# V's products taken from x * g, u written over it afterwards, and the first stage's rows, root, splits and bias sums placed anew

## The chip, the cores and the metric

The kernel runs on one core of a Trainium2 chip. The metric is the time that the device takes for one execution, in microseconds (us). Engines are named as the profile names them: PE is TensorE, PEld its weight loads, DVE VectorE, ACT ScalarE, POOL GpSimd, SP SyncE, which here only issues transfers (DMA).

## What is computed

One layer of a decoder block over 1024 tokens of width 1024. Only the start of it matters here: the normalised and modulated input `u`, its projections, and attention.

```python
def _modulate(x, g, shift, scale):
    return _rmsnorm(x, g) * (1 + scale[:, None, :]) + shift[:, None, :]
...
mod = c_act @ w_ada[l] + b_ada[l]
sh1, sc1, gt1, sh2, sc2, gt2 = jnp.split(mod, 6, axis=-1)
u = _modulate(h, g_mix[l], sh1, sc1)
...
proj = u @ w_in
q, k, v, us, g_att, g_ssm = jnp.split(proj, ...)
```

Three attention patterns with a softmax over the keys follow, an S5 branch, gates, an output projection, and a gated MLP. With r the inverse root mean square of a token and g = g_mix * (1 + scale), u = x * g * r + shift. So u @ W = r * ((x * g) @ W) + shift @ W: a product with x * g can be scaled by r per token afterwards, and the shift adds one row, the same for all tokens. The weights of a softmax sum to one, so such a row in V adds itself unchanged to the output of attention.

## The kernel before

Every float32 matrix product is done as three products of reduced-precision parts: high times high, high times low, low times high (`mm3`, L188 to L192). So each operand is split into a high part (ScalarE, a copy) and a low part (VectorE or POOL, a subtraction).

**First products.** `xT` is x with channels on partitions, in eight tiles of 128 channels (`xs[k]`). For each k, `xg[k]` is x * g in two parts. g needs the row products of the conditioning vector with `w_ada` (`row_dot`, L1502, one VectorE row per 128 outputs). The first products take 128 columns each of q, k and the two thirds of `us` (seven tiles in PSUM, `b0`: four columns groups, two halves of 512 tokens, less one) from `xg`, k by k, with the weights `w0` (L416 to L453).

**Root.** x by token (`xn`, eight blocks) is squared and summed on ScalarE (L356). `root` (L394) makes r from it; `spread_a` and `spread_b` (L406 to L414) spread r along the free axis with diagonal tiles and a product with -1 (L413), so `rr` holds -r (signs cancel in what follows).

**Shift row.** The eight `row_dot`s for the shift stand in the table `DOTS` among the first products; `shl` holds the shift in two parts, and 16 short products with `w0` (L494, L495) give shift @ W for q, k and us.

**u and V.** `u_half` makes u for one k and half: VectorE (L1480), ScalarE for the high part (L1481), VectorE for the low part (L1486). V's products follow, tokens as rows: for each half (`hf`) and each k, four tiles of 128 tokens, 12 products, 192 in all. In the first half u is made one k ahead; in the second half u's second half is made, and the q and k tiles are scaled, biased and split (`put_q`, `put_k`), and V's tiles of the first half are emptied (`put_v`: four ScalarE rows, L531, and four VectorE rows, L534, for each tile of 128 tokens). The four tiles of the second half follow, then the `us` tiles (`put_us`, L568).

**Attention** then runs with a fill of further projections from u; its first fill products take a PSUM bank that V's fifth tile must have left. Weights for these go through `Weights` (L70 to L140): one load buffer, a high part on ScalarE, and a low part on POOL (L121) for the first ones.

**Order.** The program is recorded by hand in the order of this code; each engine runs its rows strictly in that order and waits by semaphore. `b.unit(us)` moves a clock that lets spawned generators issue their next piece. SP's transfers are one queue in program order too.

Of the kernel before, what the change touches and what calls it, by code (L numbers as in the profile page):

```python
# [16 lines left out]
P = 128  # L17
# [35 lines left out]
DOTS = ((4, 5), (5, 1), (5, 4), (6, 0), (6, 2), (6, 4), (6, 6), (7, 1))  # L53
# [16 lines left out]
class Weights:  # L70
# [25 lines left out]
    def _split_to(self, n):  # L96
        b, nc = self.b, self.b.nc
        while self.ns < min(n, len(self.items)):
# [10 lines left out]
            lo = nc.vector if self.ns >= self.vec else nc.gpsimd  # L109
# [105 lines left out]
def body(tc, I, O, dbg=None):  # L215
    b = Builder(tc, I, O)
    nc = tc.nc
    with ExitStack() as ctx:
# [88 lines left out]
        def split_w(i):  # L307
            raw = raws.pop(i)
            w = b.whl.tile([P, 2, 1024], R32, name="whl", tag="whl") if i == 5 else b.A([P, 2, 1024], R32, "whA")
            nc.scalar.activation(w[:, 0], raw, AF.Copy)  # L310
            nc.vector.tensor_sub(w[:, 1], raw, w[:, 0].bitcast(F32))
            return w
# [27 lines left out]
        ssq = pg1.tile([P, 2, KT], F32, name="ssq")  # L340
# [7 lines left out]
        def load_xn(n):  # L348
            if n in (0, 2):
                page = b.A([P, 2, D], F32, "xn")  # L350
                xnp[n], xnp[n + 1] = page[:, 0], page[:, 1]
            nc.sync.dma_start(xnp[n % 4], I["xn"][n])

        def square(n):

            nc.scalar.activation(xnp[n % 4], xnp[n % 4], AF.Square, accum_out=ssq[:, 0, n:n + 1])  # L356
# [37 lines left out]
        def root(_):  # L394
# [6 lines left out]
            nc.vector.scalar_tensor_tensor(r, t, -1.5, r, op0=OP.add, op1=OP.mult)  # L401

# [12 lines left out]

        late = {}  # L416
        for fn, at in ((row_dot, DOTS), (root, ((7, 0),)), (spread_a, ((7, 2),))):
# [6 lines left out]
        for k in range(KT):  # L424
# [4 lines left out]
            if 3 <= k < 7:  # L429
                load_row(2 * k - 6)  # L430
                load_row(2 * k - 5)
            if 2 <= k < 6:
                for n in (2 * k - 4, 2 * k - 3):
                    if n > 3:
                        square(n - 4)
                    load_xn(n)
# [4 lines left out]
            elif k == 6:  # L441
                for n in range(4, KT):
                    square(n)
                load_w(4)
                load_w(5)
            o = (k % 2) * 512
            for n, ((t, hf), ps) in enumerate(b0.items()):
# [3 lines left out]
                b.mm3(ps, w[:, 0], w[:, 1], xg[k][:, 0, halves[hf]], xg[k][:, 1, halves[hf]], k == 0, k == KT - 1)  # L451
                b.unit(0.65)
            del xg[k]  # L453
        spread_b(0)
# [3 lines left out]
        u = []  # L458
        t0 = {}
        for e in range(2):  # L460
            page = b.A([P, 4, HF], F32, "t0")
            for j in range(4):
                t0[2 * e + j // 2, j % 2] = page[:, j]
        del page

        def scale_r(*ii):
            for i in ii:
                nc.vector.tensor_mul(t0[i], b0.pop(i), rr[:, halves[i[1]]])
# [9 lines left out]
        def u_half(k, hf, *between):  # L478
            u_a(k, hf)
            scale_r(*between)  # L480
            u_b(k, hf)
# [1507 lines left out]
```

## Time and profile before

| | us |
|---|---|
| three timed runs | 1149.85, 1153.71, 1154.62 |
| their median | 1153.71 |
| profiled execution, whole | 1151.12 |
| its span in the profile | 1149.3 |
| TensorE busy | 1108.6 (96%) |
| VectorE busy | 866.3 (75%) |
| ScalarE busy | 583.2 (51%) |
| POOL busy | 149.6 (13%) |
| granted TensorE clock, mean | 0.99 |

A row of a timeline gives start, length, engine, line, operation, tiles written and read, and in brackets the idle time ahead of it with what ended it. Rows of one engine overlap a little: the next may start before the last has ended. "x4" are four rows in one. TensorE's busy time counts modelled ends of overlapping products, so that a share of 96% doesn't mean that it is never behind.

### The profile page before, as it was taken

How to read it: one execution, taken by the hardware profiler on the slowest of the kernel's cores; microseconds unless marked ns; L12 is line 12 of the kernel's file. 1: busy time of each engine (PE TensorE's matmuls, PEld its weight loads, DVE VectorE, ACT ScalarE, POOL GpSimd, SP SyncE). 2: the span in 40 equal slices, each digit the busy share in tenths (PEclk: the TensorE clock that was granted, in tenths of full speed). 3: DMA queues.
4: the chain of work that ended last, by engine and by line, in shares of the span. 5: the costliest groups of instructions: out<-in, count | busy, mean ns of one | idle time of the engine just before them, and what ended most of it. 6: DMA issues, size and time to landing. Idle time of an engine off the chain costs nothing.

```text
span 1149.3 us, 14742 instructions
## 1 busy us (share of the span) xinstructions
PE 1108.6 (96%) x5286; PEld 912.2 (79%) x5286; DVE 866.3 (75%) x1656; ACT 583.2 (51%) x1065; POOL 149.6 (13%) x171
## 2 busy tenths in 40 slices
PE   9799999999999999999799999999999999999995
PEld 8667888888878887878678887788888888887784
DVE  6678687876569597378686879888877677879876
ACT  3648777778832312243233665443444346636653
POOL 1001444445422222000000000000000000000003
PEclk9999999999999999999999999999999999999998
DMA  9811111111022122245484362245423327779433
GB/s 366 351 55 56 63 39 38 47 46 65 11 72 85 49 83 64 65 137 185 163 316 148 104 238 73 92 152 203 139 92 129 128 92 274 251 265 386 142 128 147
DMA packets 57337, 159.20 MB, mean 139 GB/s; under 512 B 7440, under 2 KB 13712, under 8 KB 55472
## 3 DMA queue, kind: packets, MB, share of 16 engines
q1 hardware_dynamic: 47520, 144.56, 35.2%
q10 hardware_dynamic: 9744, 13.70, 3.8%
q8 instruction: 41, 0.67, 0.2%
q14 instruction: 32, 0.26, 0.1%
HBM read 126.20 MB, written 31.46 MB: 137 GB/s over the span
## 4 chain that ended last, share of the span: by engine, by line
PE 62%; DVE 14%; DMA 8%; ACT 8%; issue 8%; POOL 1%; SPq 0%; POOLq 0%; ACTq 0%; DVEq 0%
PE ps_s L1333 10%; PE ps_mm L1333 9%; PE ps_mm L190 7%; PE ps_t L1333 7%; PE ps_mm L192 7%; PE ps_mm L191 7%; PE ps_s L192 2%; PE ps_s L190 2%; PE ps_s L191 2%; DMA xn<-in_xn 2%; PE ps_t L1641 2%; PE ps_s L1605 1%; PE ps_o L1658 1%; PE ps_s L1606 1%; DMA x<-in_xT 1%
## 5 line engine op out<-in xcount | busy, mean ns | idle before, releaser
L1333 PE MATMUL ps_s<-op,half 128*128 128x512 f32 x792 | 189.6, 390 | 4.0 <-ACT ps_s L1347 2.9
L1333 PEld LDWEIGHTS ps_s<-op,half 128*128 128x128 f32 x792 | 148.3, 188 | 36.5 <-ACT ps_s L1347 3.9
L190 PE MATMUL ps_mm<-u,whl 128*128 128x512 f32 x360 | 144.9, 402 | 3.2 <-ACT sg L744 2.0
L192 PE MATMUL ps_mm<-u,whl 128*128 128x512 f32 x360 | 141.6, 393 | 0.0
L191 PE MATMUL ps_mm<-u,whl 128*128 128x512 f32 x360 | 141.1, 392 | 0.0
L1333 PE MATMUL ps_mm<-op,half 128*128 128x512 f32 x528 | 125.2, 389 | 0.0
L1333 PEld LDWEIGHTS ps_mm<-op,half 128*128 128x128 f32 x528 | 99.1, 188 | 20.6
L1333 PE MATMUL ps_t<-op,half 128*128 128x512 f32 x432 | 103.9, 389 | 0.7 <-ACT tp L1341 0.7
L1333 PEld LDWEIGHTS ps_t<-op,half 128*128 128x128 f32 x432 | 81.0, 188 | 17.9 <-ACT tp L1341 1.1
L121 POOL TENSOR_TENSOR whl<-wraw,whl 128x256 fp32r<-128x256 f32 (+2 forms) x52 | 62.1, 1196 | 208.1 <-ACT whl L118 208.1
L1447 POOL TENSOR_TENSOR hh<-hh,acc 128x512 f32<-128x512 f32 x3 | 4.3, 1454 | 650.9 <-ACT acc L1436 650.9
L190 PEld LDWEIGHTS ps_mm<-u,whl 128*128 128x128 f32 x360 | 68.2, 189 | 15.3 <-ACT sg L744 2.5
L192 PEld LDWEIGHTS ps_mm<-u,whl 128*128 128x128 f32 x360 | 67.9, 189 | 15.4 <-DVE whl L121 0.3
L191 PEld LDWEIGHTS ps_mm<-u,whl 128*128 128x128 f32 x360 | 68.3, 190 | 10.5
L1646 DVE TENSOR_TENSOR PT<-ps_t,PT 128x512 fp32r<-128x512 f32 (+1 forms) x80 | 50.6, 633 | 28.2 <-ACT PT L1644 27.7
L1139 DVE TENSOR_TENSOR half<-scr,half 128x512 fp32r<-128x512 f32 x80 | 54.5, 684 | 16.2 <-ACT half L1138 16.1
L118 ACT ACTIVATE whl<-wraw 128x256 fp32r<-128x256 f32 (+2 forms) x72 | 48.7, 676 | 28.3 <-PE ps_s L192 14.6
L1617 ACT ACTIVATE S<-S,mcol 128x128 f32<-128x128 f32 (+3 forms) x64 | 49.3, 771 | 14.5 <-DVE mcol L1615 12.9
L1621 POOL TENSOR_SCALAR S<-S,mcol 128x128 f32<-128x128 f32 (+3 forms) x64 | 48.7, 764 | 49.8 <-DVE mcol L1620 35.6
L1138 ACT ACTIVATE half<-scr 128x512 fp32r<-128x512 f32 x80 | 49.0, 625 | 8.7 <-DVE scr L1120 5.6
L1139 DVE TENSOR_TENSOR half<-wraw,half 128x512 fp32r<-128x512 f32 x66 | 45.0, 685 | 8.0 <-ACT half L1138 7.9
L1644 ACT ACTIVATE PT<-ps_t 128x512 fp32r<-128x512 f32 (+1 forms) x80 | 43.8, 551 | 10.5 <-PE ps_t L1641 9.4
(516 smaller groups left out, 2424.7 us busy)
## 6 DMA issues: line engine op xcount, KB each, us to landing
wraw<-in_wup SPq DMA_DIRECT2D x32, 512.0 KB, 3.6
fq<-f SPq DMA_DIRECT2D x16, 1024.0 KB, 5.3
ft<-fq SPq DMA_DIRECT2D x14, 1024.0 KB, 7.7
ada<-in_wada SPq DMA_DIRECT2D x24, 512.0 KB, 8.9
wraw<-in_wdn SPq DMA_DIRECT2D x20, 512.0 KB, 5.8
adaB<-in_wada ACTq DMA_DIRECT2D x16, 512.0 KB, 4.5
wraw<-in_wout SPq DMA_DIRECT2D x16, 512.0 KB, 3.7
hd<-h SPq DMA_DIRECT2D x12, 512.0 KB, 7.3
```

The lines of the kernel that those rows point to most:

```text
L118: nc.scalar.activation(w[:, 0, cs], raw[:, cs], AF.Copy)
L121: lo.tensor_sub(w[:, 1, cs], raw[:, cs], w[:, 0, cs].bitcast(F32))
L190: nc.tensor.matmul(ps, wh, xh, start=first, stop=False)
L191: nc.tensor.matmul(ps, wh, xl, start=False, stop=False)
L192: nc.tensor.matmul(ps, wl, xh, start=False, stop=last)
L1138: nc.scalar.activation(w[:, 0], src, AF.Copy)
L1139: lows.append(lambda: nc.vector.tensor_sub(w[:, 1], src, w[:, 0].bitcast(F32)))
L1333: mm = lambda wp, xp, i: nc.tensor.matmul(ps, w[:, wp, ws], xp[:, cs], start=first and k + i == 0, stop=k == KT // 2 - 1 and i == 2, skip_ ...
L1617: nc.scalar.activation(tl, tl, AF.Exp, bias=mc[:, 0:1], scale=-1.0, accum_out=mc[:, 2:3])
L1621: nc.gpsimd.tensor_scalar(tl, tl, mc[:, 3:4], 0.0, op0=OP.mult, op1=OP.add)
L1644: nc.scalar.activation(pt[:, 0, :w], tps[:, :w], AF.Copy)
L1646: 0, lambda: nc.vector.tensor_sub(pt[:, 1, :w], tps[:, :w], pt[:, 0, :w].bitcast(F32)))
```

## The change

1. V's products read `xg[k]` and not u. So they can start when the first products end. `put_v` scales each tile by r per token: ScalarE's copy takes `scale=ssq[:, 2, t]` (a column, r with the sign that it needs, one small row more in `root`), VectorE's subtraction becomes a `scalar_tensor_tensor` with the same column. The shift's part of V is a row of its own: `rows_of("v", wv)`, 16 more short products, transposed into the columns `vb`, added in attention where the two halves of an output are summed.
2. `u` is the same memory as `xg`. `gen_u`, spawned, writes each k and half after V's products have read it (`taken`).
3. The seven PSUM tiles of the first products are copied to SBUF by ScalarE as they end (`keep`), so that V's tiles get these banks; the scaling by r then works on the copies.
4. Loads: the blocks of x by token come without a wait for each other (four pages in place of two), ahead of the shift's rows. V's first weight is loaded and split among the first products. `DOTS` keeps four of the eight row dots; four move into V's first half, with the two spreads, the scaling, the shift and both `rows_of`.
5. The low parts of the first two weights for attention go to VectorE, not POOL. Of the `us` tiles, three are written among V's last emptyings, bias and layout in one row.

```diff
-DOTS = ((4, 5), (5, 1), (5, 4), (6, 0), (6, 2), (6, 4), (6, 6), (7, 1))
+DOTS = ((6, 1), (6, 4), (7, 2), (7, 4))
+U_PACE = 1.5
...
-            lo = nc.vector if self.ns >= self.vec else nc.gpsimd
+            lo = nc.vector if self.ns >= self.vec or self.ns < 2 else nc.gpsimd
...
+            nc.vector.tensor_scalar(ssq[:, 2], r, -1.0, None, op0=OP.mult)
...
+        def keep(i, ps):
+            if not t0_pages:
+                t0_pages.extend(b.A([P, 4, HF], F32, "t0") for _ in range(2))
+            t0[i] = t0_pages[i[0] // 2][:, 2 * (i[0] % 2) + i[1]]
+            nc.scalar.activation(t0[i], ps, AF.Copy)
...
-        for fn, at in ((row_dot, DOTS), (root, ((7, 0),)), (spread_a, ((7, 2),))):
+        for fn, at in ((row_dot, DOTS), (low4, ((7, 0),)), (root, ((7, 1),)), (spread_a, ((7, 5),)), (more_rows, ((6, 6),))):
...
+            for n in {2: (0, 1), 3: (2, 3), 4: (4, 5), 5: (6, 7)}.get(k, ()):
+                load_xn(n)
+            for n in {4: (0, 1), 5: (2, 3), 6: (4, 5)}.get(k, ()):
+                square(n)
+            if k == 5:
+                load_w(4)
+            for n in {5: (0, 1), 6: (2, 3)}.get(k, ()):
+                load_row(n)
...
+                if k == KT - 1:
+                    keep((t, hf), ps)
...
+        u = [xg[k] for k in range(KT)]
...
+        def gen_u():
+            last = None
+            for hf in range(2):
+                for k in range(KT):
+                    while (k, hf) not in taken:
+                        yield 0.6
+                    u_a(k, hf)
+                    if last:
+                        u_b(*last)
...
+                    last = k, hf
+                    yield U_PACE
...
+        def rows_of(n, ws, tag="o"):
+            ps = b.ps(tag)
+            for k in range(KT):
+                o = (k % 2) * 512
+                w = ws[k // 2][:, :, o:o + 512]
+                nc.tensor.matmul(ps[0:2], shl[:, k], w[:, 0], start=k == 0, stop=False)
+                nc.tensor.matmul(ps[0:1], shl[:, k, 0:1], w[:, 1], start=False, stop=k == KT - 1)
+                b.unit(0.43)
+            brow[n] = b.tp()
+            nc.scalar.activation(brow[n][0:2], ps[0:2], AF.Copy)
...
-                nc.scalar.activation(V[p][:, t, :, 0:HD], src[:, 2 * p:2 * p + 2], AF.Copy)
-            yield
+                nc.scalar.activation(V[p][:, t, :, 0:HD], src[:, 2 * p:2 * p + 2], AF.Copy, scale=ssq[:, 2, t:t + 1])
+            yield 1.4
...
-                nc.vector.tensor_sub(V[p][:, t, :, HD:P], src[:, 2 * p:2 * p + 2], V[p][:, t, :, 0:HD].bitcast(F32))
+                nc.vector.scalar_tensor_tensor(V[p][:, t, :, HD:P], src[:, 2 * p:2 * p + 2], ssq[:, 2, t:t + 1],
+                                               V[p][:, t, :, 0:HD].bitcast(F32), op0=OP.mult, op1=OP.subtract)
...
+                nc.scalar.activation(o, t0.pop((2 + m, hf)).rearrange("p (j t) -> p t j", t=T), AF.Identity,
+                                     bias=bias0[:, 2 + m:3 + m])
...
+                    if k == 1:
+                        load_w(7)
+                        spread_b(0)
+                        spread_a(1)
+                        row_dot(4)
+                        scale_r((1, 0))
+                        row_dot(5)
+                    if k == 2:
+                        spread_b(1)
+                        wv.append(split_w(6))
+                        row_dot(6)
+                        scale_r((2, 0))
+                        row_dot(7)
+                        shift()
+                        b.spawn(gen_u(), 0.5)
+                    if k == 3:
+                        scale_r((0, 0))
+                    if k == 4:
+                        rows_of("u", w0)
...
+                    if k == 6:
+                        scale_r((2, 1))
+                        rows_of("v", wv)
...
-                    if k + 1 < KT:
-                        u_b(k + 1, 1)
-                    next(put)
-                    if k + 2 < KT:
-                        u_a(k + 2, 1)
-                    list(put)
-                    xs[k] = None
-                    if k == 3:
-                        us0 = [(t - 2, hf, add_bias0(t, hf)) for t, hf in ((2, 0), (2, 1), (3, 0))]
+                    b.spawn(put)
+                    if k in (4, 5, 6):
+                        put_us(*((0, 0), (0, 1), (1, 0))[k - 4])
...
-            nc.vector.tensor_add(t[hp, 256:512], o[0:64, 0:256], t[0:64, 0:256])
+            nc.vector.scalar_tensor_tensor(t[hp, 256:512], o[0:64, 0:256], vb[0:64, 2 * p + h2:2 * p + h2 + 1], t[0:64, 0:256],
+                                           op0=OP.add, op1=OP.add)
```

Line numbers shift by the change: the spread's product is L413 before and L416 after, u's three rows are L1480, L1481, L1486 before and L1542, L1543, L1548 after, V's are L531 and L534 before and L567 and L570 after.

On TensorE, the end of the first products (the last tile, `ps_o`) and what follows it before (`tp,nones` is the spread, `shl` the shift, `ps_s` V's first tile):

```order
L190 MATMUL ps_o<-xg,whA 128x512
L191 MATMUL ps_o<-xg,whA 128x512
L192 MATMUL ps_o<-xg,whA 128x512
L413 MATMUL ps_o<-tp,nones 128x512
L494 MATMUL ps_o<-whl,shl 2x512
L495 MATMUL ps_o<-whl,shl 1x512
```

and with the change, from the same place on:

```order
L191 MATMUL ps_o<-xg,whA 128x512
L192 MATMUL ps_o<-xg,whA 128x512
L193 MATMUL ps_o<-xg,whA 128x512
L191 MATMUL ps_s<-whA,xg 128x512
L192 MATMUL ps_s<-whA,xg 128x512
L193 MATMUL ps_s<-whA,xg 128x512
```

V's products stand directly behind the first products now; the spread comes after V's first step of twelve, the shift's row after the fourth.

On VectorE, the emptying of V at the end of V's products before (`V<-` are V's rows, tiles 2 to 7 in banks t, mm and o; `u` and `x` rows make u; the last row is attention's first score):

```order
L534 TENSOR_TENSOR V<-ps_s,V 128x2x64 x4
L1486 SCALAR_TENSOR_TENSOR u<-x_103,mod,u 128x512
L534 TENSOR_TENSOR V<-ps_t,V 128x2x64 x8
L534 TENSOR_TENSOR V<-ps_mm,V 128x2x64 x8
L534 TENSOR_TENSOR V<-ps_o,V 128x2x64 x8
L1608 ISA S_939,mcol<-ps_s,near 128x128
```

and with the change (`xg` is u now, `whl<-wraw` a weight's low part for attention):

```order
L570 SCALAR_TENSOR_TENSOR V<-ps_t,ssq,V 128x2x64 x4
L122 TENSOR_TENSOR whl<-wraw,whl 128x1024
L1542 SCALAR_TENSOR_TENSOR x_102<-x_102,gs_115,rr 128x512
L1548 SCALAR_TENSOR_TENSOR xg<-xk,mod,xg 128x512
L570 SCALAR_TENSOR_TENSOR V<-ps_t,ssq,V 128x2x64 x4
L570 SCALAR_TENSOR_TENSOR V<-ps_mm,ssq,V 128x2x64 x8
L1542 SCALAR_TENSOR_TENSOR x_103<-x_103,gs_115,rr 128x512
L1548 SCALAR_TENSOR_TENSOR xg<-x_102,mod,xg 128x512
L1548 SCALAR_TENSOR_TENSOR xg<-x_103,mod,xg 128x512
L570 SCALAR_TENSOR_TENSOR V<-ps_o,ssq,V 128x2x64 x8
L1670 ISA S_970,mcol<-ps_s,near 128x128
```

A weight's split and the rows of u's last tiles now stand among V's last emptyings.

More of the change, by code (lines that the diff above doesn't have):

```diff
@@ L308, in split_w @@
             raw = raws.pop(i)
-            w = b.whl.tile([P, 2, 1024], R32, name="whl", tag="whl") if i == 5 else b.A([P, 2, 1024], R32, "whA")
+            w = b.whl.tile([P, 2, 1024], R32, name="whl", tag="whl") if i == 7 else b.A([P, 2, 1024], R32, "whA")
             nc.scalar.activation(w[:, 0], raw, AF.Copy)
@@ L441, in body @@
             elif k == 6:
-                for n in range(4, KT):
+                for n in (6, 7):
                     square(n)
-                load_w(4)
+                w4 = split_hi(4)
+                wv = [w4[0]]
                 load_w(5)
@@ L502, in body @@
[L502 to L513 removed]
+        taken = set()
@@ new lines, in gen_u @@
+        def gen_u():
[7 more added lines that the diff above has]
+                        u_b(*last)
+                    if last and last[1]:
+                        xs[last[0]] = None
+                    last = k, hf
+                    yield U_PACE
+            yield 0.7
+            u_b(*last)
+            xs[last[0]] = None
@@ new lines, in bias_cols @@
+        def bias_cols(n, width, out, tag="o"):
+            cps = b.ps(tag)
+            row = brow.pop(n)
+            for t in range(HF // width):
+                nc.tensor.transpose(cps[:width, 2 * t:2 * t + 2], row[0:2, t * width:(t + 1) * width], ident[0:2, 0:2])
+            bcp = b.tp()
+            m = 2 * HF // width
+            nc.scalar.activation(bcp[:width, :m], cps[:width, :m], AF.Copy)
+            yield 2.0
+            nc.vector.tensor_add(out[:width], bcp[:width, 0:m:2], bcp[:width, 1:m:2])
@@ L615, in body @@
                 vps += [b.ps(t) for t in ("mm", "mm", "o", "o")]
+        for t in (4, 5):
+            list(put_v(t))
+        b.drain()
+        for t in (6, 7):
+            list(put_v(t))
         p1.close()
@@ L625, in body @@
         W.prefetch(1)
-        for t in range(4, 8):
-            list(put_v(t))
-        for x in us0:
-            put_us(*x)
-        t0.clear()
-        del us0, x
+        assert not t0
         def U(k, hf):
@@ L693, in body @@
         W.slow = True
-        attention(b, V, QK, Oat, pS, near, far, ident, mcol, fill)
+        attention(b, V, QK, Oat, pS, near, far, ident, mcol, vb, fill)
         W.finish()
@@ L1570, in s5_coefficients, with attention @@
     v.tensor_scalar(AA[64:P, 1], AA[64:P, 1], -1.0, None, op0=OP.mult)
-def attention(b, V, QK, Oat, pS, near, far, ident, mcol, fill):
+def attention(b, V, QK, Oat, pS, near, far, ident, mcol, vb, fill):
     nc = b.nc
```

110 lines of the change are left out of this document (44 added, 66 removed).

## The prediction

> **What bounds the kernel now.** I read the busy time by stage first, with stages cut where TensorE's work changes.
>
> ```profile
> core 0: us, PE busy (x) PEld busy (x) DVE busy (x) ACT busy (x) POOL busy (x), PEclk, DMA share, GB/s
> 49.20:61.67 12.47, 6.66 (x20) 2.06 (x19) 6.52 (x14) 6.94 (x14) 0.00 (x0) 0.73 0.39 148
> 61.67:109.20 47.53, 46.09 (x199) 36.23 (x197) 39.28 (x68) 30.52 (x64) 3.71 (x2) 1.00 0.11 38
> 109.20:332.00 222.80, 218.46 (x1281) 186.16 (x1280) 153.82 (x464) 167.50 (x367) 99.14 (x132) 1.00 0.15 50
> ```
>
> The third row is attention: TensorE is busy for 98% of it, so a shift of its start reaches the end of the kernel nearly whole. Nothing behind it is changed in order. The second row is V's products. The first row is the gap between the first products and V's, which the change goes for. The timeline of TensorE gives its length, the waits what ends it:
>
> ```profile
> 48.98 0.39 PE L192 MATMUL ps_o<-xg,whA 128*128 128x512 f32 x1
> 54.48 2.08 PE L413 MATMUL ps_o<-tp,nones 128*128 128x512 f32 x2 [5.12 <-ACT tp L408]
> 61.67 0.40 PE L190 MATMUL ps_s<-whA,u 128*128 128x512 f32 x1
> 61.90 0.39 PE L191 MATMUL ps_s<-whA,u 128*128 128x512 f32 x1
> ...
> 65.96 1.02 PE L413 MATMUL ps_o<-tp,nones 128*128 128x512 f32 x2
> ...
> 110.34 0.47 PE L190 MATMUL ps_mm<-u,whl 128*128 128x512 f32 x1 [1.14 <-DVE V L534]
> ```
>
> A product starts 0.228 us after the one before it (61.67, 61.90). First products end at 48.98 + 0.23 = 49.2, V's start at 61.67: **12.5 us** apart, filled by the wait for the root, its spread over the partitions (L413) and 16 short products for the bias row (L494, L495). At 110.34 TensorE restarts for attention, held 1.14 us by VectorE's emptying of V's bank. **110.34 is the time to beat.**
>
> **The change on TensorE.** V's products now read x * g, which lies there, so they start at 49.2. They are 2 x 8 steps of 12: 192 x 0.2275 = 43.7. The two spreads move inside: 0.9 each (two passes; the row at 65.96 ran undisturbed). The bias row's 16 products stay and 16 more come for V's own shift row: 32 x 0.23 = 7.4. Small transposes: about 0.6. With no wait TensorE ends V at 49.2 + 43.7 + 1.8 + 7.4 + 0.6 = 102.7 and restarts, after the 1.2 that emptying the last bank cost before, at 103.9. That is **6.4 us earlier than 110.34**, the most the change can give. The extra row eats 3.7 of the gap.
>
> **Inputs.** SP's order is equal up to the last x, and then the eight blocks of x by token come before the rows for the shift.
>
> ```profile
> 25.53 1.56 SPq L297 DMA_DIRECT2D ada<-in_wada  x2
> 32.99 1.57 SPq L352 DMA_DIRECT2D xn<-in_xn  x2
> 39.12 1.57 SPq L352 DMA_DIRECT2D xn<-in_xn  x2
> 48.57 1.06 ACT L356 ACTIVATE xn<-xn 128x1024 f32<-128x1024 f32 x1 [3.23 <-DMA xn<-in_xn]
> 50.82 1.28 ACT L397 ACT_TABLE_LOAD   x1
> 50.99 1.23 DVE L1502 CUSTOM_DVE_ANT_0 ada<-ada,cpage 128x1024 f32<-128x1024 f32 x1 [3.01 <-DMA ada<-in_wada]
> 58.17 1.23 DVE L311 TENSOR_TENSOR whA<-wvx,whA 128x1024 fp32r<-128x1024 f32 x1 [3.36 <-ACT whA L310]
> ```
>
> Blocks of 512 KB go out every 1.24 us (six from 25.53 to 32.99) and land 9.5 us later (39.12 to 48.57). The six blocks of x by token that remain take the places from 25.53 on, so the last goes out at 31.7 and lands near 41.2; before, it landed near 49.7. The squares end near 44. The first V weight lands next (42.5), and VectorE has split it by 47.8; the table load and root sit between the seven bank copies that ScalarE now makes. None of this holds TensorE at 49.2. The next limit is VectorE: between 48.5 and the shift it has six row dots and two splits, with two root copies and the second spread of ScalarE in between. Laid end to end (a dot 1.2 and a split 1.14, as rows overlap the next by 0.08; two scalings 0.62; the shift's three small rows 0.6; waits for ScalarE's splits 3.2) the shift is ready at **63.1**. TensorE reaches the shift row at 49.2 + 4 x 2.73 + 1.8 = 62.0, so it waits **1.1**. If the last of these loads take the full 9.5 us after issue, 0.6 more. V's first half, with all that lies in it, then ends at 82.0, the second at 103.8 on TensorE.
>
> **The change on VectorE and ScalarE.** This decides. u is now made behind V's products, 16 tiles of 128x512, each a VectorE row, a ScalarE row and a VectorE row; before, it was made ahead of them. I count with these rows of VectorE's timeline (start, length):
>
> ```profile
> 59.31 0.75 DVE L1480 SCALAR_TENSOR_TENSOR xk<-xk,gs,rr 128x512 f32<-128x512 f32 x1
> 59.98 0.68 DVE L468 TENSOR_TENSOR t<-ps_s,rr 128x512 f32<-128x512 f32 x1
> 80.49 0.75 DVE L1480 SCALAR_TENSOR_TENSOR x<-x,gs,rr 128x512 f32<-128x512 f32 x1
> 82.69 0.75 DVE L1480 SCALAR_TENSOR_TENSOR xk<-xk,gs,rr 128x512 f32<-128x512 f32 x1
> 87.89 0.68 DVE L546 SCALAR_TENSOR_TENSOR QS<-t,QS 64x512 fp32r<-64x512 f32 x1
> 94.93 0.42 DVE L561 CAST KH<-KH 64x512 fp32r<-64x512 f32 x1
> 109.32 1.66 DVE L534 TENSOR_TENSOR V<-ps_mm,V 128x128 fp32r<-128x128 f32 x8
> ```
>
> and these of ScalarE's, then two groups by line and form (busy time, mean ns of one) and POOL's split:
>
> ```profile
> 53.15 1.28 ACT L408 ACTIVATE tp<-ident,ssq 128x128 f32<-128x128 f32 x4 [0.49 <-DVE ssq L401]
> 56.60 0.60 ACT L414 ACTIVATE rr<-ps_o 128x512 f32<-128x512 f32 x1 [2.17 <-PE ps_o L413]
> 88.37 0.73 ACT L1481 ACTIVATE u<-xk,mod 128x512 fp32r<-128x512 f32 x1
> 89.00 0.71 ACT L519 ACTIVATE t<-t,bias 128x512 f32<-128x512 f32 x1
> 89.74 0.63 ACT L543 ACTIVATE QS<-t 64x512 fp32r<-64x512 f32 x1
> 99.74 1.05 ACT L118 ACTIVATE whl<-wraw 128x1024 fp32r<-128x1024 f32 x1
> 100.69 0.75 ACT L531 ACTIVATE V<-ps_s 128x128 fp32r<-128x128 f32 x4
> 110.88 2.51 ACT L568 ACTIVATE usr<-t 128x512 f32<-128x512 f32 x2
> L408 ACT ACTIVATE tp<-ident,ssq 128x128 f32<-128x128 f32 x8 | 2.5, 389 | 0.5 <-DVE ssq L401 0.5
> L531 ACT ACTIVATE V<-ps_s 128x128 fp32r<-128x128 f32 x8 | 1.5, 283 | 0.0
> 100.87 2.41 POOL L121 TENSOR_TENSOR whl<-wraw,whl 128x1024 fp32r<-128x1024 f32 x1 [95.71 <-ACT whl L118]
> ```
>
> In the second half ScalarE first waits for the last tile of the first half to be read (82.0), with the query rows queued behind it, so VectorE idles from about 80.7 to 83.5. From there to the emptying of the bank that TensorE needs for its restart, VectorE owes 14 u rows at 0.67, the step from 59.31 to 59.98 (9.4), eight 64x512 rows at 0.70 (5.6), four copies at 0.43 (1.7), twenty V rows at 0.21 (4.2), and two weight splits at 1.14 that were POOL's at 2.41 (2.3): 23.2, so 106.7 if it never waits. By the starts from 88.37 to 89.74, ScalarE owes 8 u rows at 0.63 and four biases at 0.74; further eight 64x512 copies at 0.66, two splits at 1.0, three us tiles at 1.25 (before these came after V, at 110.88), and twenty V pieces.
>
> A V piece now has a per-token scale read from a column. The same rows without one start 0.16 apart ((0.75 - 0.28) / 3, four rows less the mean of one); the spread's 128x128 rows, which have one, 0.30 ((1.28 - 0.39) / 3). Of 128x512, the bias add with a column takes 0.71, the copy without 0.60. So **a column costs 0.11 to 0.14**; I take 0.29 a piece, the ends being nothing extra and 0.16. That makes ScalarE's sum 5.0 + 3.0 + 5.3 + 2.0 + 3.8 + 5.8 = 24.9 from 82.1: 107.0. The Trainium skill, ScalarE: Activation LUTs, section What ACT_TABLE_LOAD costs, has a column operand add about 93 ns to an ACTIVATE; by that rule twenty pieces cost 1.9 instead of 2.6 and the sum below is 0.3 earlier. The rows give a little more, and the rule speaks against this change as they do.
>
> Neither engine runs its sum through: each u tile passes VectorE, ScalarE, VectorE, and from the fourth step on four V pieces stand between. Step by step in the order built, a tile with its V pieces costs 2.9 (VectorE's row 0.75, ScalarE's 0.63, four pieces 1.17, VectorE's last piece 0.3) and some handing over, and 4.8 where the second weight split falls (ScalarE 0.95 from 99.74 to 100.69, VectorE 1.14, in part side by side). VectorE ends the last key row at 97.8, V's tiles 0, 1, 2 at 98.7, 101.6, 104.8, the second split at 106.7, tile 3 at 109.6 and tile 4, the bank in question, at 110.8. TensorE restarts at **110.9, 0.6 later than before**. Without the column's cost the same walk ends at 109.0, 1.3 earlier than before; with 0.16 it ends 0.9 later.
>
> The other parts are covered. The bank copies (seven at 0.5) lie beside the last first products and the first four V products. In attention the sum with V's column replaces an add of the same 64x256; 32 of them at 0 to 0.07 more lie beside TensorE.
>
> ```profile
> 115.04 0.29 DVE L1608 CUSTOM_DVE_ANT_0 S<-ps_s,near 128x128 f32<-128x128 f32 x1 [2.47 <-DMA near<-in_bt]
> SPq L92 <- POOL whl L121: 27.4, 2, 23.8
> ```
>
> Scores began at 115.04, held by the bias table, which SP sent late because a weight load ahead of it waited for POOL. VectorE's split frees that buffer near 106.7, so the table is in time; but VectorE ends V near 116, so the first score comes some 1 us later than before, inside the lead that attention's products give.
>
> **Rivals.** *TensorE bound*: the emptying keeps up, and restart comes near 105, with the wait of 1.1 in it. Against it stands VectorE's own sum, 106.7. Price -5.3 on the mean of 1152.3 (below): 1147.0. *Slower*: u's loop is not overlapped. When nothing stood between, a tile took 2.20 (80.49 to 82.69) where VectorE's two rows need 1.34; if ScalarE, late behind V pieces, holds VectorE for 0.86 at each of the eight second-half tiles, restart comes 6.9 later than I have it: 1159.8; at half of them 1156. It decides as soon as ScalarE's row ends after VectorE's rows between. *It doesn't do what it says*: V's start waits, for a bank or a split, 2 us or more; as V's end hangs on VectorE and ScalarE, most of that is lost again: 1153 to 1155.
>
> **How the numbers follow.** The profiled run took 1151.12, 1.8 around its span of 1149.3; the three timed runs' median is 1153.71, and all four executions' mean is 1152.3. On this one execution the sum is 1151.7; on the mean 1152.9, which I give, and no change against the median. Forecast 0.70, TensorE bound 0.12, slower loop 0.12, late start 0.06. The forecast's own range is -3 to +3, the bounds of the column (-1.3), the loads (+0.6) and the first scores (+1), with the runs' own spread of 2 each side: 1148.5 to 1157. Taking in most of the TensorE-bound case, 1147.5 to 1157.5. Against 0.5% of 1153.71, 5.8 us, about what a measurement of this kernel can tell from no change: two thirds of each outer rival's chance falls past the bounds of 1147.9 and 1159.5: faster 0.09, same 0.83, slower 0.08.
>
> **What would show it.** V's first product near 49.2; TensorE idle about 1 us ahead of the shift row; no idle in V's second half, then **6 to 7 us of idle ahead of attention's first product**, put down to VectorE's V rows; V pieces on ScalarE about 0.29 apart; first score near 116. An idle there under 3 us would make me wrong towards faster, over 9 towards slower.

## The result: slower by 0.5%, and the profile after

The changed kernel takes 1157.32 us (median of 12 runs, 1155.44 to 1160.06), the kernel before 1151.39 on the same chip (12 runs). The ratio is 1.0050, with a 95% interval of 1.0042 to 1.0058: 5.9 us slower. The time lies just inside the upper end of the range (1157.5); the forecast, 1152.9 and no change, was wrong. The profiled execution has a span of 1154.4, 5.1 over the one before.

Line numbers from here on are those of the changed kernel: L567 and L570 are V's high and low pieces, L1542, L1543 and L1548 the three rows of a u tile, L1670 a score on VectorE, L1679 an exponential on ScalarE, L1732 VectorE's sum at the end of a job of attention. TensorE's timeline of the changed kernel:

```profile
49.47 0.39 PE L191 MATMUL ps_s<-whA,xg 128*128 128x512 f32 x1
...
63.22 0.40 PE L534 MATMUL ps_o<-whl,shl 128*2 128x512 f32 x1 [0.94 <-DVE shl L526]
...
104.24 0.39 PE L193 MATMUL ps_o<-whA,xg 128*128 128x512 f32 x1
112.69 0.77 PE L191 MATMUL ps_mm<-xg,whl 128*128 128x512 f32 x1 [8.06 <-DVE V L570]
113.25 0.63 PE L192 MATMUL ps_mm<-xg,whl 128*128 128x512 f32 x1
113.68 0.63 PE L193 MATMUL ps_mm<-xg,whl 128*128 128x512 f32 x1
114.10 0.63 PE L191 MATMUL ps_mm<-xg,whl 128*128 128x512 f32 x1
```

The gap ahead of V is gone, V starts near 49.4, the wait for the shift is 0.94, and V's last product goes out at 104.24, four and a half us ahead of before. Then TensorE idles for 8.06 and restarts at 112.69 instead of 110.34, and its first products follow each other some 0.43 us apart instead of 0.23. The windows (length, busy times, granted clock in the third column from the end) show that clock:

```profile
104.40:112.69 8.29, 0.23 (x3) 0.03 (x1) 5.89 (x16) 5.91 (x19) 0.00 (x0) 0.77 0.29 95
112.69:114.60 1.91, 1.91 (x5) 1.52 (x6) 1.91 (x6) 0.27 (x1) 0.00 (x0) 0.50 0.06 13
115.90:117.60 1.70, 1.70 (x9) 1.36 (x8) 1.49 (x6) 1.21 (x5) 0.00 (x0) 1.00 0.00 0
```

The first score and the first exponential, on VectorE and ScalarE after the change:

```profile
116.11 2.16 DVE L570 SCALAR_TENSOR_TENSOR V<-ps_o,ssq,V 128x128 fp32r<-128x128 f32 x8 [0.28 <-ACT V L567]
118.40 0.29 DVE L1670 CUSTOM_DVE_ANT_0 S<-ps_s,near 128x128 f32<-128x128 f32 x1
...
118.78 1.28 ACT L1679 ACT_TABLE_LOAD   x1 [1.67 <-DVE mcol L1670]
120.07 0.40 ACT L1679 ACTIVATE S<-S,mcol 128x128 f32<-128x128 f32 x1
```

and before the change, the load of ScalarE's table and the same exponential:

```profile
115.06 1.28 ACT L1617 ACT_TABLE_LOAD   x1
116.35 0.40 ACT L1617 ACTIVATE S<-S,mcol 128x128 f32<-128x128 f32 x1
```

The score is 3.36 later than before, directly behind V's last low row and no longer held by the bias table; the exponential is 3.72 later. The other 0.36 lies between the two. Before, the table load began at 115.06, behind ScalarE's last us tile and before the first score had ended (115.33). Now ScalarE ends V at 117.11, stands idle for 1.67 until the score is done, and loads its table only then. No run here loads it earlier.

From the first exponential to the last of attention's 32 sums the kernel before took 209.36 us, this one 210.33. So the span's 5.1 are **3.72 up to the first exponential, 0.97 in attention, and 0.4 behind it**. Behind the last sum the same code took 822.7 to 826.6 in the profiles below, so one span alone can't place a single us there. The first exponential varies from execution to execution too: V's first product starts between 48.2 and 49.7 in the changed kernel and its variants, two kernels that are the same up to attention (changed, e6) have exponentials 0.45 apart, and two others (before, e15) 1.15. So a step of half a us in the table below shows nothing by itself.

### The profile page after: what moved, and what is told of

It reads as the page before. It is cut to its first block, busy times and chain, and to the rows that moved or that the text cites. A ratio compares the mean times of both kernels' runs of the same rounds, so it can differ in the third digit from the quotient of the medians.

```text
span 1154.4 us, 14821 instructions
## 1 busy us (share of the span) xinstructions
PE 1113.2 (96%) x5310; PEld 916.7 (79%) x5310; DVE 871.4 (75%) x1660; ACT 588.1 (51%) x1071; POOL 144.5 (13%) x169
## 4 chain that ended last, share of the span: by engine, by line
PE 71%; DVE 13%; issue 7%; ACT 6%; DMA 2%; POOL 1%; POOLq 0%; SPq 0%; ACTq 0%; DVEq 0%
PE ps_s L1395 12%; PE ps_mm L1395 8%; PE ps_t L1395 8%; PE ps_mm L191 7%; PE ps_mm L193 7%; PE ps_mm L192 7%; PE ps_s L191 3%; PE ps_s L193 3%; PE ps_s L192 3%; PE ps_t L1703 2%; PE ps_s L1667 1%; PE ps_o L1720 1%; PE ps_s L1668 1%; DVE op L952 1%; DVE x L1025 1%
## 5 line engine op out<-in xcount | busy, mean ns | idle before, releaser
L191 PE MATMUL ps_mm<-xg,whl 128*128 128x512 f32 x368 | 147.9, 402 | 10.1 <-DVE V L570 8.1
L193 PE MATMUL ps_mm<-xg,whl 128*128 128x512 f32 x368 | 144.4, 392 | 0.0
L192 PE MATMUL ps_mm<-xg,whl 128*128 128x512 f32 x368 | 144.2, 392 | 0.0
L191 PEld LDWEIGHTS ps_mm<-xg,whl 128*128 128x128 f32 x368 | 69.7, 189 | 22.5 <-ACT V L567 8.5
L193 PEld LDWEIGHTS ps_mm<-xg,whl 128*128 128x128 f32 x368 | 69.4, 189 | 15.6 <-DVE whl L122 0.3
L192 PEld LDWEIGHTS ps_mm<-xg,whl 128*128 128x128 f32 x368 | 69.8, 190 | 10.9
L122 POOL TENSOR_TENSOR whl<-wraw,whl 128x256 fp32r<-128x256 f32 (+2 forms) x50 | 57.3, 1146 | 107.0 <-ACT whl L119 107.0
L1679 ACT ACTIVATE S<-S,mcol 128x128 f32<-128x128 f32 (+3 forms) x64 | 49.3, 771 | 14.2 <-DVE mcol L1677 12.7
```

Of the source, the lines that this page charges most:

```text
L122: lo.tensor_sub(w[:, 1, cs], raw[:, cs], w[:, 0, cs].bitcast(F32))
L191: nc.tensor.matmul(ps, wh, xh, start=first, stop=False)
L192: nc.tensor.matmul(ps, wh, xl, start=False, stop=False)
L193: nc.tensor.matmul(ps, wl, xh, start=False, stop=last)
L1679: nc.scalar.activation(tl, tl, AF.Exp, bias=mc[:, 0:1], scale=-1.0, accum_out=mc[:, 2:3])
```

## The experiments

The table gives for each kernel the start of the first exponential and the time from it to the last sum of attention (both from the timelines), and the time over that of the kernel before on the same chip. From e1 on, each but the last is the changed kernel with the edit named.

| kernel | first exp | to last sum | ratio to before, 95% interval |
|---|---|---|---|
| before | 116.35 | 209.36 | 1 |
| changed | 120.07 | 210.33 | 1.0050 (1.0042 to 1.0058) |
| e1 high pieces ahead | 119.86 | 210.74 | 1.0064 (1.0051 to 1.0077) |
| e2 tiles 4, 5 first | 118.25 | 210.23 | 1.0033 (1.0020 to 1.0045) |
| e3 TensorE kept busy | 120.00 | 210.31 | 1.0046 (1.0034 to 1.0059) |
| e4 splits on POOL | 120.71 | 210.32 | 1.0065 (1.0052 to 1.0079) |
| e5 no shift row of V | 116.57 | 210.70 | 1.0031 (1.0019 to 1.0043) |
| e6 no column in the sum | 119.62 | 210.00 | 1.0045 (1.0033 to 1.0057) |
| e7 V between scores | 114.58 | 218.44 | 1.0075 (1.0060 to 1.0089) |
| e8 no token scale | 117.98 | 210.60 | 1.0042 (1.0030 to 1.0054) |
| e9 e2, row between halves | 117.75 | 210.28 | 1.0034 (1.0022 to 1.0046) |
| e10 e9, low rows late | 116.19 | 210.36 | 1.0014 (1.0006 to 1.0023) |
| e11 e10, less waiting | 115.22 | 210.39 | 1.0001 (0.9992 to 1.0009) |
| e12 e11, column on ScalarE | 114.85 | 210.31 | 1.0007 (0.9998 to 1.0015) |
| e13 e11, row's copies on VectorE | 113.55 | 210.25 | **0.9983 (0.9974 to 0.9991)** |
| e14 e13, tile 6 late | 112.39 | 211.04 | 0.9986 (0.9977 to 0.9995) |
| e15 kernel before, longer sum | 117.50 | 210.07 | 1.0017 (1.0008 to 1.0025) |

### Is it the restart?

The first theories: A, the loss is the late restart (2.35) and the slow clock behind it; B, it lies in the added rows of TensorE and of attention; C and D, A's parts are made up again before the end.

e3 fills TensorE's idle time, so that only the slow clock goes.

```
+        wps = b.ps("s")
+        for _ in range(34):
+            nc.tensor.matmul(wps, u[0][:, 0, 0:P], u[0][:, 0, 0:HF], start=True, stop=True)
```

> 34 products of 128x512 that nobody reads are put into the idle time ahead of attention's first product (34 x 0.227 = 7.7 us, 104.6 to 112.3). Theory A (after 8 us of idle the first seven products go every 0.43 us, that is worth 1.4): restart unmoved near 112.7, products at once 0.23 apart, first score's product near 116.2 instead of 117.61, time near 1156.0. Rival D (what the clock costs is made up in attention's lead): time within 0.4 of 1157.3.

Its TensorE timeline:

```profile
104.39 7.87 PE L680 MATMUL ps_s<-xg 128*128 128x512 f32 x34
112.61 0.47 PE L191 MATMUL ps_mm<-xg,whl 128*128 128x512 f32 x1 [0.36 <-DVE V L570]
112.92 0.39 PE L192 MATMUL ps_mm<-xg,whl 128*128 128x512 f32 x1
...
116.13 0.22 PE L1671 MATMUL ps_s<-KH,QS 128*128 128x128 f32 x1
118.68 0.45 PE L1671 MATMUL ps_s<-KH,QS 128*128 128x384 f32 x1 [0.56 <-DVE mcol L1674]
```

The first score's product comes at 116.13 instead of 117.61, as theory A had it. But VectorE makes the score at 118.33, as in the changed kernel (118.40), the exponential stays at 120.00, and TensorE gives the time back waiting for it. So in the changed kernel neither the slow clock nor TensorE's first 15 products decide, as rival D says (its time, 1156.62, is 0.3 below D's bound, but the two ratios' intervals overlap). The margin is small: the first score's products ended at 117.94 in the changed kernel, V's last low row at 118.27.

e1 and e2 change the order of the emptying.

```
-                    b.spawn(put)
+                    b.spawn(put, 0.0 if k < 4 else next(put))
```

> Only ScalarE's order changes: the four high V pieces of tiles 0 to 3 go ahead of the u row of the same step. Theory A (the emptying of V is a ring: VectorE's first u row, ScalarE's u row, ScalarE's four high pieces, VectorE's four low pieces, next u row, 3.66 us a turn, 101.92 to 105.58): without the high pieces in the ring a turn is ScalarE's own work, near 3.0, so three turns give 2.0: restart for attention near 110.7 instead of 112.69, idle ahead of it 6.1, time near 1155.3. Theory B (the loss comes from the extra rows of V's shift, 3.7 on TensorE, and the longer sums in attention): restart may move, the time stays within 0.5 of 1157.3.

```
-                        else put_v(k - 4)
+                        else put_v(k - 4) if k < 6 else iter(())
...
-        for t in (6, 7):
+        for t in (2, 3, 6, 7):
             list(put_v(t))
...
-        W.prefetch(1)
+        W.prefetch(2)
```

> V's tiles 4 and 5, whose banks attention's first products need, are emptied ahead of tiles 2 and 3, and the second weight split goes behind all of V. Theory A: tile 4 is empty some 2 to 3 us after V's last product (104.6), restart near 107, idle under 3 us, products at 0.23 us apart from the first one: time near 1150.5, 6.8 below the changed kernel (5.5 for the restart, 1.3 for the clock) and a little below the kernel before. Rival C (the first scores decide, not the restart: VectorE still has the same rows to do, so V ends near 118 and the first score near 118.5 as now): time above 1156. Theory B: within 0.5 of 1157.3.

Theory A's times fail on both. e1's restart comes at 111.75, 0.94 earlier where 2.0 were expected, and 0.79 of that is an earlier start of V in that execution. VectorE now waits 1.53 for the high part of the second weight split instead. e1 also shows the other side of e3. VectorE ended V at 117.34, 0.93 sooner than in the changed kernel, and then had to wait for TensorE, where twelve of the fourteen steps between the first 15 products were 0.43 or longer:

```profile
118.19 0.29 DVE L1670 CUSTOM_DVE_ANT_0 S<-ps_s,near 128x128 f32<-128x128 f32 x1 [0.85 <-PE ps_s L1668]
```

So its first exponential is only 0.21 earlier. In e2 TensorE restarts at 107.89, 4.8 earlier than in the changed kernel, and the first exponential moves by 1.82, the last sum by 1.92: the time follows the scores and not the restart, as rival C says, though the first score did move (116.59) and 1154.76 is 1.2 under its bound. In the whole table the step from the first exponential to the last sum is 210.0 to 210.7 whatever the restart, save for e7 and e14, which put the most work between the scores, and the kernel before. This became theory F: **attention ends a fixed time after its first exponential**.

### What makes the first exponential late?

e5 leaves out V's shift row, e8 the column of V's pieces, e4 gives POOL its two splits back.

```
-                        rows_of("v", wv)
+                        nc.vector.memset(vb, 0.0)
```

> The shift row of V, its transposes and its bias sum are left out (V lacks the shift's share, vb is zero). Theory F (attention runs a fixed time after its first exp, and the first exp comes when VectorE and ScalarE have ended V; ScalarE's first work of the second half waits for TensorE at 79.4 and 82.7, so the row's 3.7 us of TensorE go into that chain): V's first half ends some 4 us earlier, ScalarE and VectorE start the second half 2.5 to 4 earlier, first exp near 117 instead of 120.07, time 1154.0. Theory A2 (the chain of the second half is limited by VectorE's and ScalarE's own work only, TensorE is 12 us off): first exp moves under 0.8, time above 1156.5.

```
-                nc.scalar.activation(V[p][:, t, :, 0:HD], src[:, 2 * p:2 * p + 2], AF.Copy, scale=ssq[:, 2, t:t + 1])
+                nc.scalar.activation(V[p][:, t, :, 0:HD], src[:, 2 * p:2 * p + 2], AF.Copy)
```

(and VectorE's row a plain `tensor_sub`)

> V is emptied without the token scale (left out: V lacks it): ScalarE's copy without a column, VectorE's plain difference. Each group of four pieces should take 0.75 instead of 1.12 on ScalarE and 0.88 instead of 1.13 on VectorE. In the ring of tiles 1 to 3 that is 0.6 a turn, for tiles 4 to 7 0.25 each on VectorE: V ends on VectorE 2.5 to 3 earlier, first exp near 117.3. Theory F: time 1154.6. Theory A2 (restart decides): restart 2 earlier, 1155.3. If neither place decides: 1157.3.

```
-            lo = nc.vector if self.ns >= self.vec or self.ns < 2 else nc.gpsimd
+            lo = nc.vector if self.ns >= self.vec else nc.gpsimd
```

> The first two low weight splits go back from VectorE to POOL (2.4 us each there). Theory A: VectorE is spared 1.15 twice, the second between tiles 2 and 3 on the way to the restart; restart 111 to 111.7, time 1155.6 to 1156.5. Rival E (the bias table, queued on SP behind the weight load that waits for POOL, then comes later and holds the first scores): restart earlier, first score still at 118 or later, time 1157.3 or above.

Without the row the first exponential comes 3.50 earlier and the time is 1153.83, as theory F has it (by the ratios the gain is 2.2, as the kernel before was faster on that chip). Without the column the exponential comes 2.09 earlier, but the time, 1155.71, is a us above theory F and nearer to A2's 1155.3. The rows of e8 show why:

```profile
109.75 0.77 PE L191 MATMUL ps_mm<-xg,whl 128*128 128x512 f32 x1 [5.89 <-DVE V L570]
112.58 1.67 DVE L570 TENSOR_TENSOR V<-ps_o,V 128x128 fp32r<-128x128 f32 x8
116.31 0.29 DVE L1669 CUSTOM_DVE_ANT_0 S<-ps_s,near 128x128 f32<-128x128 f32 x1 [2.06 <-PE ps_s L1667]
```

VectorE ended V at 114.25, 4.0 sooner than in the changed kernel (0.8 of that is an earlier start of V in this execution), and then stood for 2.06: TensorE restarted at 109.75, and thirteen of its fourteen steps were 0.42 or longer. So the restart and its clock do decide as soon as VectorE is more than a little faster. e2 and e7, e9 to e14, which restart at 107.9 or before, have no such wait.

e4 goes against theory A and, in its restart of 113.33, against rival E too: all is later, the exponential by 0.64 (1.46 counted from V's first product, which was earlier here). Its rows on POOL and VectorE say why:

```profile
93.56 2.92 POOL L122 TENSOR_TENSOR whl<-wraw,whl 128x1024 fp32r<-128x1024 f32 x1 [88.41 <-DVE xk L1542]
94.25 2.52 DVE L600 CAST KH<-KH 64x512 fp32r<-64x512 f32 x1
106.27 2.34 POOL L122 TENSOR_TENSOR whl<-wraw,whl 128x1024 fp32r<-128x1024 f32 x1 [9.79 <-ACT whl L119]
106.32 2.83 DVE L1542 SCALAR_TENSOR_TENSOR x<-x,gs,rr 128x512 f32<-128x512 f32 x1
```

A copy of 0.42 and a u row of 0.75 last until 0.3 and 0.5 us after POOL's split has ended. A split on POOL costs VectorE 2.1 us here, one of its own 1.15. So by the rows this part of the change is a gain; the ratios, 1.0065 and 1.0050, have intervals that overlap.

### Attention's own 0.97

e6 takes V's column out of the sum, e12 (on e11) gives it to ScalarE, e15 puts the longer sum alone into the kernel before.

```
-            nc.vector.scalar_tensor_tensor(t[hp, 256:512], o[0:64, 0:256], vb[...], t[0:64, 0:256], op0=OP.add, op1=OP.add)
+            nc.vector.tensor_add(t[hp, 256:512], o[0:64, 0:256], t[0:64, 0:256])
```

> In attention V's column of the shift is not added (the output lacks it): the sum of 64x256 is again an add of two tensors, 32 of them. Between the first and the last of these sums the changed kernel takes 194.1 us, the kernel before 193.1. Theory G (the longer sum, 0.06 each on VectorE, costs that 1.0): 193.1 again, first exp unmoved at 120.07, time 1156.3. Theory H (the 1.0 comes from the order of attention's other work): 194.1, time 1157.3.

```
-            nc.scalar.activation(t[0:64, 0:256], o[64:128, 0:256], AF.Copy)
+            nc.scalar.activation(t[0:64, 0:256], o[64:128, 0:256], AF.Identity, bias=vb[64:128, ...])
```

(with e6's sum)

> As that, and V's column of the shift is added by ScalarE's copy of the upper half of a product (a bias column) instead of by VectorE's sum, which is a sum of two tensors again. Theory G (the longer sum costs 0.7 to 1.0 over attention): first sum to last 193.1 to 193.6 instead of 194.1, time 0.5 to 1 under the one before, 1151 to 1152, at or below the kernel before. Rival (a bias column costs ScalarE as much there): the same time as without.

```
-            nc.vector.tensor_add(t[hp, 256:512], o[0:64, 0:256], t[0:64, 0:256])
+            nc.vector.scalar_tensor_tensor(t[hp, 256:512], o[0:64, 0:256], b.zcol[0:64, 0:1], t[0:64, 0:256], op0=OP.add, op1=OP.add)
```

> The kernel before, with one edit: attention's sum of 64x256 is the longer form, with a column of zeros. Theory G: first sum to last 193.8 to 194.2 instead of 193.1, end and time 0.7 to 1.0 later, 1152.2. Theory H (the 1.0 comes from how attention's other work stands in the changed kernel): 193.1, time within 0.3 of the kernel before.

e6 has 193.40 from the first sum to the last against 194.14, e15 193.87 against 193.15: theory G, 0.7 of the 0.97. From the first exponential to the last sum e6 gains only 0.33 (210.00 against 210.33), while e15 loses the whole 0.71 (210.07 against 209.36); how much of it reaches the end in the changed kernel is not shown. By lines, the sum takes 416 ns without and 475 with a column (e15):

```profile
L1672 DVE SCALAR_TENSOR_TENSOR tp<-ps_o,zcol,tp 64x256 f32<-64x256 f32 x32 | 15.2, 475 | 15.9 <-ACT tp L1671 15.5
```

e12 keeps 194.11, as its rival had it: the column costs ScalarE 0.09 a copy (472 against 381 ns) and attention as much. The ratio of e15 is +0.17%, its profile's first exponential also 1.15 late, in an execution whose spread ahead of V waited 1.34 longer (6.46 against 5.12); that is not the edit's, and the time alone would not have told 0.7.

### V's row, the scores, and a version that beats both

e7 moves work behind the first scores.

```
+        b.spawn(put_v(6), 5.0)
+        b.spawn(put_v(7), 7.0)
+        b.spawn(split_late(), 3.5)
         attention(
```

> As the one that emptied tiles 4 and 5 first, and tiles 6 and 7 (needed only by attention's sums of products) and the second weight split go behind the first scores. Theory F: VectorE is free for the first score at 113.4 instead of 116.59, first exp near 115 instead of 118.25, last sum of attention some 3 earlier than there; what is put between the scores may cost 1 of it: time 1151.5 to 1152.5, level with the kernel before or a little below. Theory A2 (the end of V on VectorE does not decide): time near 1154.8 as there.

The first exponential is at 114.58 as expected, and the rest is wrong: 218.44 to the last sum, and a time of 1158.76. ScalarE's V pieces and its quarters of the weight split stood between the exponentials, and VectorE's quarters waited for ScalarE's. ScalarE's rows, then VectorE's:

```profile
115.47 0.40 ACT L119 ACTIVATE whl<-wraw 128x256 fp32r<-128x256 f32 x1
117.45 1.12 ACT L567 ACTIVATE V<-ps_o,ssq 128x128 fp32r<-128x128 f32 x4
...
113.18 0.42 DVE L1677 CUSTOM_DVE_ANT_0 S<-ps_s,near 128x256 f32<-128x256 f32 x1
115.90 0.42 DVE L122 TENSOR_TENSOR whl<-wraw,whl 128x256 fp32r<-128x256 f32 x1 [2.29 <-ACT whl L119]
...
119.61 0.43 DVE L122 TENSOR_TENSOR whl<-wraw,whl 128x256 fp32r<-128x256 f32 x1 [1.87 <-ACT whl L119]
```

So theory F fails where work that waits for another engine stands between the scores; e14 below loses a little there even without such a wait. e9 to e14 keep every computation. e9 issues V's row between V's halves; e10 adds that only low rows, whose high rows are done, go behind the scores; e11 sorts the emptying so that ScalarE works while VectorE empties tile 4.

```
                 del xnp
-                vps += [b.ps(t) for t in ("mm", "mm", "o", "o")]
+                vrow = rows_of("v", wv, False)
+                vps += [b.ps(t) for t in ("mm", "mm")]
```

(e9: and the row's copy, its transposes and the "o" banks ahead of the product of tile 6 in the next step)

> On the order that empties tiles 4 and 5 first: V's shift row is issued between V's two halves instead of ahead of the first half's last two steps, and its copy on ScalarE behind the first query rows. All work is done. Theory F (attention's end follows the first exp, and what ScalarE's second half waits for at 79.4 and 82.7 is TensorE's first half): the chain starts up to 3.5 earlier, but the late u rows then wait for V's own products again (2.73 a step), so 2 to 3.5 of it stays: first exp at 115 to 116.3 instead of 118.25, time 1151.5 to 1153.0, within 0.2% of the kernel before. If the row's place did not matter: 1154.8.

```
-        for t in (2, 3, 6, 7):
+        for t in (2, 3, 6):
             list(put_v(t))
+        v7 = put_v(7)
+        next(v7)
...
+        W.lag = 4.6
         W.prefetch(2)
+        b.spawn(v7, 3.6)
```

> As that, and the low rows of V's tile 7 and of the second weight split stand on VectorE behind the second and the fourth score; their high rows stay on ScalarE ahead of the first exp. Theory F with the sum of VectorE's work (what stands between scores costs only where VectorE has no gap; the gaps between the first five scores were 0.94, 0.33 and 0.73): the first score comes 2.2 earlier than there, half of it or more is kept: time 1150.3 to 1152, not above the kernel before. Rival (as when tiles 6 and 7 stood between the exps: each change of engine costs again 1 to 2): 1153 or more.

```
+        pv = {t: put_v(t) for t in range(2, 8)}
+        for t in (4, 5, 2):
+            next(pv[t])
+        list(pv[4])
         b.drain()
+        for t in (5, 2, 3, 6):
+            list(pv[t])
```

(e11: and tile 1's high pieces ahead of a us tile)

> On the kernel with the late low rows (first exp 116.19, ScalarE without a gap ahead of it): ScalarE makes tile 2's high pieces while VectorE makes tile 4's low ones, tile 5's low pieces go behind the last u row, and tile 1's high pieces go ahead of a us tile. ScalarE's idle 1.9 (for VectorE's last first u row) should shrink under 0.5, VectorE's 0.79 go. Theory F: first score 113.0 to 113.6 instead of 113.97, first exp 114.3 to 115, last sum of attention 1.2 to 1.9 earlier, time 1151.8 to 1152.5. If attention no longer follows the first exp at this point: time 1153.7.

e9 gained 0.5, not 2 to 3.5, and nothing in time (1.0034 against e2's 1.0033). ScalarE's timeline shows it standing at the row's copies with the second query queued behind them:

```profile
79.99 0.63 ACT L583 ACTIVATE QS<-t 64x512 fp32r<-64x512 f32 x1
81.59 0.59 ACT L673 ACTIVATE tp<-ps_o 2x512 f32<-2x512 f32 x1 [0.98 <-PE ps_o L535]
83.31 0.18 ACT L549 ACTIVATE tp<-ps_o 64x16 f32<-64x16 f32 x1 [1.13 <-PE ps_o L546]
83.52 0.72 ACT L557 ACTIVATE t<-t,bias 128x512 f32<-128x512 f32 x1
```

e10 and e11 moved the first score as theory F says (113.97 and 113.55); e11's exponential is 0.2 past its range, e10's time is 1.7 above its range, e11's 0.7 below. e13 leaves the row where e9 has it and takes those waits off ScalarE.

```
-                        nc.scalar.activation(brow["v"][0:2], vrow[0:2], AF.Copy)
+                        b.drain(put)
+                        nc.vector.tensor_copy(brow["v"][0:2], vrow[0:2])
```

(likewise the second copy; and `next(put)` at once for the second query and the keys)

> On the kernel with less waiting (first exp 115.22, level with the kernel before): V's shift row stays between the halves, but its two copies are VectorE's, behind the first query's rows, and ScalarE's query and key copies go ahead of the u row of the step. Theory P (what V's row costs is ScalarE's standing still for TensorE, 0.98 and 1.13 at its copies, and VectorE behind it, 2.27): ScalarE has the second query ready 2 to 3 earlier, V ends 1.5 to 3 earlier, first exp 112.5 to 113.7, time 1148.3 to 1150. Theory Q (the row's 3.7 us on TensorE cost it, wherever its copy stands): first exp near 115.2, time 1151.2 as there.

```
-        for t in (5, 2, 3, 6):
+        for t in (5, 2, 3):
...
+        b.spawn(v6, 3.6)
```

(e14: tile 7's low rows and the second split's come later too, at 4.4 and 6.0 instead of 3.6 and 4.6)

> As that, and tile 6's low rows too stand behind the second score. Theory F: the first score 1.0 earlier, of which what stands between scores takes back up to half: 0.3 to 1 less time than without. Rival (TensorE's first score product, 15 products behind its restart, or ScalarE's table load now decides): the same within 0.3.

e13's ScalarE has the second query done at 83.1, where e9's had not begun it:

```profile
81.82 0.63 ACT L586 ACTIVATE QS<-t 64x512 fp32r<-64x512 f32 x1
82.47 0.63 ACT L587 ACTIVATE QS<-t 64x512 fp32r<-64x512 f32 x1
85.08 0.73 ACT L1563 ACTIVATE xg<-xk,mod 128x512 fp32r<-128x512 f32 x1 [1.98 <-PE ps_o L193]
```

Theory Q fails and theory P's forecast holds: the exponential is 1.67 earlier than e11's (1.1 counted from V's first product), with the row's products unchanged on TensorE. Its two edits were not run apart, so how much is due to the copies and how much to the order is not shown. The time, 1150.16, is 0.2 above P's range and, by the ratios, **0.17% under the kernel before and 0.7% under the changed one**. e14's exponential is 1.16 earlier still, but 0.79 of it is lost again between the scores, and the time is the same: the forecast of 0.3 to 1 less fails. The rival's number comes out, but not for its reason, as the first score did come 1.15 earlier.

## Why the prediction was wrong, point by point

- **First stage.** V's start at 49.2, the shift's wait of 1.1 (0.94 measured) and V's end at 103.8 on TensorE (104.24) came as said, and so did VectorE's idle time (said 80.7 to 83.5, found 81.1 to 84.0).
- **The failing step: "the first score comes some 1 us later than before, inside the lead that attention's products give".** There is no such lead. e2, e3 and e5 show that attention follows the first exponential nearly one for one, so a later first score had to be counted in full. The first score came 3.4 later and not 1: V ended on VectorE at 118.27, where the prediction had it near 116. Of these 2.3, 1.7 had gathered when tile 4 was empty (112.5 against 110.8), the rest behind it. With the 0.36 ahead of the exponential, 0.97 in attention and 0.4 behind it, these are the 5.1. "110.34 is the time to beat" and the share of 98% for TensorE led there: a busy TensorE at the restart does 15 products and then waits for scores. The restart's 2.35 cost nothing in the changed kernel (e3), but only because VectorE was later still; in e8 it held the first score for 2.06.
- **The walk of VectorE and ScalarE** had the order right and the price of a tile wrong, 2.9 "and some handing over". These rows of VectorE and ScalarE after the change are one turn:

```profile
101.92 1.13 DVE L570 SCALAR_TENSOR_TENSOR V<-ps_s,ssq,V 128x128 fp32r<-128x128 f32 x4 [0.78 <-ACT V L567]
102.96 0.74 DVE L1542 SCALAR_TENSOR_TENSOR xk<-xk,gs,rr 128x512 f32<-128x512 f32 x1
...
103.80 0.72 ACT L1543 ACTIVATE xg<-xk,mod 128x512 fp32r<-128x512 f32 x1 [0.74 <-DVE xk L1542]
104.43 1.12 ACT L567 ACTIVATE V<-ps_t,ssq 128x128 fp32r<-128x128 f32 x4
...
105.58 1.13 DVE L570 SCALAR_TENSOR_TENSOR V<-ps_t,ssq,V 128x128 fp32r<-128x128 f32 x4 [1.22 <-ACT V L567]
```

  Low rows, the next u row, ScalarE's u row, its four high pieces, low rows again: a ring of 3.66. VectorE's first low row waits for the last of the four high pieces (105.55), where the walk let it follow piece by piece. With the second split the turn was 4.80, as predicted. TensorE's idle time ahead of attention became 8.06 and not 6 to 7.
- **The column** on ScalarE costs 0.09 a piece (360 against 272 ns in e8, banks s and t), less than the 0.13 taken; but VectorE's low row costs 0.06 more too (345 against 282), which the prediction left out with 0.21 a row. Together they put V's end on VectorE 4.0 later than in e8 (3.2 counted from V's first product), of which the first exponential showed 2.1. Twenty pieces at 1.9 instead of 2.6 would take 0.7 off ScalarE's sum of 24.9, where the prediction says 0.3.
- **V's extra row** was counted on TensorE as taking 3.7 off a gap that would not be needed. It costs 3.5 at the first exponential (e5), since ScalarE's first rows of the second half wait for TensorE, and it can be had back (e13).
- **The two splits** were counted as 2.3 on VectorE. They save 0.6 at the first exponential (e4), 1.46 counted from V's first product.
- **The longer sum** of attention was said to lie beside TensorE. It costs 0.7 from the first sum to the last (e6, e15).
- The rival *slower loop* had the sign and nearly the size (1156 at half of the tiles): VectorE did stand for 0.8 to 1.2 at each of three tiles, held by ScalarE's V pieces. But it was to act through the restart; it acted through the first score.

So the 12.5 us of gap did go, and reach TensorE's last product of V as 4.6. What the end hangs on is the chain of VectorE's and ScalarE's rows in V's second half up to the first exponential, which the change lengthened, with TensorE's restart close behind it. The medians differ by 0.8 more than the two profiles; that isn't placed.

## What to carry to other kernels

Find the event that the rest of the program follows by moving several candidates apart: here nobody waited for the engine that is 98% busy at its start. When two chains end close together, taking away one shows nothing (e3), and a gain on the other is cut short (e8). Where two engines hand a tile to and fro, draw the ring and add its rows; the sum of each engine alone is a bound that the ring does not reach. When a row waits, the rows queued behind it on that engine pay: giving two small copies to the other engine, and moving forward what stood behind them, was worth 1.1 to 1.7 us at the first exponential.

## What was not expected of the hardware

- **POOL holds VectorE.** A copy and a u row on VectorE, whose tiles are all in SBUF, lasted beside a POOL split until just after its end (2.52 for 0.42, 2.83 for 0.75, both in e4), and so did a u row in the kernel before (1.55 for 0.75 at 102.27), while V's low rows, which read PSUM, were not lengthened in the kernel before (0.89 for four at 101.47, beside POOL's split of 100.87 to 103.28). The Trainium skill, SBUF — State Buffer, section SBUF: two separate sides, says that the two engines share a pair of ports as an exclusive lock for a whole instruction. By that rule such a row waits out the rest of the split, and the trace agrees: these three ended 0.3 to 0.5 us behind it.
- **The clock.** After 8.06 us of idle the products went 0.43 apart for 3 us; after 3.58 (e2) the first six products went 0.23 apart and only then eight at 0.43, with a granted clock of 0.51 from 109.36 to 112.80; after 2.68 (e11) and 1.37 (e13) none was slow. The granted clock was 0.50 for 3.41 us in e2, for 6.83 in the changed kernel and e8, and for 10.24 in e1 and e6, so one, two or three times 3.41. Two kernels that are the same up to there (changed, e6) had six and eleven slow steps. The Trainium skill, TensorE: Matmul & The Clock Gate, section Part 1: The HAM clock gate (the "warmup" mystery), has the array fall to half its clock after an idle window of about 3.4 us and come back after about 3.4 us of work. The trace agrees in size with the idle time (no fall after 2.68, one after 3.47 in e9) and with the unit of 3.41, and e2 shows that the fall can come after work has resumed.
